# A fourth room for raw up weights in a Strassen-type gated network, the fourth rounded block kept inside the normed input, and the down weights' loads moved to GpSimd's queue

## The chip, the cores and the metric

The kernel runs on one core of one Trainium2 chip. The time is device microseconds of one execution: the median of three runs is 1200.07 us (1199.22 to 1203.46). The engines are named as in the profile: PE (matrix multiplication), PEld (its weight loads), DVE (vector engine), ACT (activation engine), POOL (GpSimd) and SP (the engine that here only issues DMAs). Each of them works through its own queue in order. A DMA is issued by one of these queues; a load that has to wait for its destination to come free waits at the head of its queue, and what is queued behind it waits too.

## The reference

Two residual layers on 512 tokens of width 1024, a state-space mixer in the first and forgetting attention in the second, each followed by a gated network. The gated network is what the change touches:

```python
def conv_ffn(h, w_up, conv_w, conv_b, w_down):
    up = h @ w_up                      # 1024 -> 2 x 2816
    a, b = jnp.split(up, 2, axis=-1)
    ...
    a_conv = conv_b
    for i in range(CONV_W):            # causal, width 3
        a_conv = a_conv + ap[:, i:i + S] * conv_w[i]
    return (jax.nn.silu(a_conv) * b) @ w_down
```

Its input h is the normed and modulated residual stream; the output is scaled by a gate and added to the stream. All of it is float32.

## The kernel before, in words

**Precision.** A float32 product is made of three faster ones. Each operand is cut into a rounded part ("hi", made by ACT, line 303) and the rest ("lo", source minus hi, made by DVE, line 304; together `put_parts`), and hi·hi, hi·lo and lo·hi are added up in PSUM. So every weight that reaches PE has passed through ACT and DVE first.

**The gated network** (`ffn`, lines 621 to 698, called once per layer: `l` is 0 and 1, called the first and the second network here). The hidden width 2816 is 22 tiles of 128; tile `f` has two weight matrices of 1024 x 128, number `2f` of the convolved branch and `2f+1` of the other, 512 KB each. The normed input `x` is a pair of tiles `a_hi`, `a_lo` of 128 partitions x 8 x 512 (8 blocks of 128 channels, 512 tokens). The tiles `f` = 0 to 3 go through a plain product (`product`, PE line 320). From `f` = 4 on `quarters` (line 548) takes the two matrices together.

**`quarters`** sees the two matrices as a 2 x 2 block matrix (a11, a12 the halves of matrix `2f` along the channels, a21, a22 those of `2f+1`) and `x` as 2 x 2 (b11, b12, b21, b22: halves of the channels by halves of the tokens), and forms the result with seven block products in place of eight. Of `x` itself it multiplies b11, b21 and b22 only; b12 (channel blocks 0 to 3, tokens 256 to 511) goes in through sums that `forms_x` made once. Each product is 12 matmuls of 256 columns (PE line 588). For one `f` the helpers do this: DVE makes four sums of 512 columns (line 556, tiles `sums`), ACT and DVE cut four weight blocks into hi and lo (a11 with a12, then two pairs of sums, 1024 columns each, then a22 alone, 512 columns), ACT copies three products (line 595, `nm_h`), DVE adds four results (line 556, `nm_t`), and the gate's elementwise work follows (lines 638 to 657). The a22 block is cut into a room of its own in the network's pool, one for hi and one for lo, which the next `f` uses again. `behind(*copied)` puts the cuts of one `f` after the last copy of the `f` before on ACT.

**The down product.** The 22 tiles are worked in groups (4, 4, 5, 4, 5 in the first network, 6, 5, 6, 5 in the second). While the tiles of one group go through the up products, the down products of the group before are spread between them, about two output blocks for each `f` (line 694). Only the last group's are made at the end.

**Rooms and queues.** `raw` (line 191) loads a weight matrix. Up weights go to the ring `raw` with three rooms (`RAW`), loaded by SP's queue (line 197). A room comes free when its last reader is done: for matrix `2f` that is the fourth sum on DVE (a12 minus the second sum), for matrix `2f+1` the cut of a22 on DVE. In the first network the down weights have a ring of their own, `rawd` with two rooms, loaded by SP's queue as well (line 194); their readers are ACT line 303 and DVE line 304. In the second network they go through the ring of three with the up weights.

**Work beside it.** During the first network DVE also reduces the modulation weights of later layers (`ada_units`, line 244): 1024 columns in one instruction (line 273), from one room `ada_raw`. Its next load is issued on POOL's queue (line 259) as soon as DVE is done with the room. `tick` calls place two of these per `f`.

**Order of the work.** The library that the kernel is written in fixes the order of every engine's queue when the program is built, from its own estimate of durations, and places semaphore waits for every read after a write, write after a read and reuse of a room. `issue_after` adds wishes to that order.

The change and the prediction's steps touch `raw`, `quarters`, and through them the loads at lines 194 and 197, the cuts at 303 and 304, and the sums at 556.

Of the kernel before, what the change touches and what calls it, by code (L numbers as in the profile page):

```python
# [9 lines left out]
F32 = mybir.dt.float32  # L10
F32R = mybir.dt.float32r
# [7 lines left out]
P = 128  # L19
D = 1024  # L20
KT = D // P
# [46 lines left out]
ROOM, ASIDE, VALUES = 9 * P, 22, 16  # L68
# [7 lines left out]
def part_of(pool, shape, name, tag, bufs, aside=0):  # L76

    _, n, w = shape
    t = pool.tile([P, ROOM if bufs == WB else n * w + P], F32R, name=name, tag=tag, bufs=bufs)
    return t[:, aside:aside + n * w].rearrange("p (n w) -> p n w", w=w)  # L80


class Trunk:
# [107 lines left out]
    def raw(self, shape, src, n=0):  # L191
        if self.room:
            t = self.bgpool.tile(shape, F32, name=self.room, bufs=2)
            self.nc.sync.dma_start(t, src)
            return t
        t = self.wpool.tile(shape, F32, name="raw", tag=("raw", "w_hi", "w_lo")[n], bufs=(RAW, WB, WB)[n])
        self.loads.dma_start(t, src)
        return t
# [349 lines left out]
    def quarters(self, pool, l, f, x, finish):  # L548

        nc = self.nc  # L550
        H, N = KT // 2, S // 2
        t1, t2 = HALVES
        a, b = (self.raw([P, KT, P], self.io["w_up"][l][2 * f + j]) for j in range(2))
        a11, a12, a21, a22 = a[:, :H], a[:, H:], b[:, :H], b[:, H:]
        c, d = (pool.tile([P, 2, H, P], F32, name="sums", bufs=2) for _ in range(2))
        sub = lambda o, u, v, op=ALU.subtract: nc.vector.tensor_tensor(o, u, v, op)  # L556
        w = {}
        copied = self.copied

        def parts(src, names, *where):  # L560
            hi, lo = (
                pool.tile([P, H * P + (P if n == "w_hi" else 32)], F32R, name=n, tag="e" + n)[:, ASIDE:ASIDE + H * P].rearrange("p (n w) -> p n w", w=P)
                if where else part_of(self.wpool, [P, len(names) * H, P], n, n, WB, ASIDE)
                for n in ("w_hi", "w_lo")
            )
            with self.behind(*copied):
                self.put_parts(hi, lo, src)
            for j, n in enumerate(names):
                w[n] = hi[:, j * H:(j + 1) * H], lo[:, j * H:(j + 1) * H]

        parts(a, ("a11", "a12"))
        sub(c[:, 0], a21, a22, ALU.add)
        sub(c[:, 1], c[:, 0], a11)
        parts(c.rearrange("p n k m -> p (n k) m"), ("s1", "s2"))
        sub(d[:, 1], a11, a21)
        sub(d[:, 0], a12, c[:, 1])
        parts(d.rearrange("p n k m -> p (n k) m"), ("s4", "s3"))
        parts(a22, ("a22",), pool)
        quarter = lambda k, t: tuple(v[:, k * H:(k + 1) * H, t] for v in x)
        xs = {"b11": quarter(0, t1), "b21": quarter(1, t1), "b22": quarter(1, t2)}  # L580
        for n, v in self.tx.items():
            xs[f"t{n}"] = v

        def times(o, wn, xn, first=True):
            (whi, wlo), (xhi, xlo) = w[wn], xs[xn]
            for k in range(H):
                for n, (wt, xt) in enumerate(((whi, xhi), (whi, xlo), (wlo, xhi))):
                    self.last_mm = nc.tensor.matmul(  # L588
                        o, wt[:, k], xt[:, k], start=(first and k == 0 and n == 0), stop=(k == H - 1 and n == 2),
                        skip_group_check=True,  # L590
                    )

        def copy(o, last=False):
            t = self.tmp.tile([P, N], F32, name="nm_h", bufs=4)
            a = nc.scalar.activation(t, o, AF.Copy)  # L595
            if last:
                self.copied = [a.ins]
            return t

        p1, p5 = (self.mm.tile([P, S], F32, name="mmp")[:, :N] for _ in range(2))  # L600
        p2, p4 = (self.aux.tile([P, S], F32, name="aux")[:, :N] for _ in range(2))
        oa, ob = (self.tmp.tile([P, S], F32, name="nm_t") for _ in range(2))
        times(p1, "a11", "b11")
        c1 = copy(p1)
        times(p5, "s1", "t1")
        c5 = copy(p5)
        times(p2, "a12", "b21")
        sub(oa[:, t1], p2, c1, ALU.add)
        times(p1, "s2", "t2", False)
        c2 = copy(p1, True)  # L610
        times(p5, "s4", "b22", False)
        sub(oa[:, t2], p5, c2, ALU.add)
        finish(2 * f, oa, slice(0, S))
        times(p4, "a22", "t4")
        c4 = copy(p4)
        times(p1, "s3", "t3", False)
        sub(ob[:, t2], p1, c5, ALU.add)
        sub(ob[:, t1], p1, c4)
        finish(2 * f + 1, ob, slice(0, S))
# [98 lines left out]
class Ew:  # L718
# [29 lines left out]
    def sub(self, a, b, out=None):  # L748
        return self.tt(a, b, ALU.subtract, out)
# [70 lines left out]
class S5(Trunk):  # L820
# [345 lines left out]
    def s5(self, i, nxt):  # L1166
# [7 lines left out]
        with ExitStack() as stack:  # L1174
# [120 lines left out]

            yhi = ylo = None
            raw, hi, lo, gps = {}, {}, {}, {}

            def part_hi(m):
# [597 lines left out]
```

## Time and profile before

| what | value |
|---|---|
| median of the runs (lowest to highest) | 1200.07 us (1199.22 to 1203.46) |
| the profiled execution's own time | 1197.47 us |
| its span, first to last instruction | 1195.7 us |
| PE busy | 1174.6 us (98%), 7983 matmuls |
| DVE busy | 1011.1 us (85%), 1836 instructions |
| ACT busy | 619.9 us (52%), 1186 instructions |
| POOL busy | 124.1 us (10%), 230 instructions |
| moved by DMA | 182.02 MB, mean 152 GB/s |

How to read it: times of views are microseconds from the start of the span. Matmuls overlap, so their durations add up to more than the span; a PE that is busy is not proof that it runs at its peak, but an idle PE is lost time. In the view of waits each row says which instruction waited for which, how long in total, how often, and the longest. In the view by windows each row is one stretch of time with the busy time of each engine in it (in brackets the number of instructions), the share of its clock that PE was granted, the share of the DMA engines and the rate. In the timeline a row is start, duration, engine, line, operation, output and inputs, and in square brackets the idle time before it and what ended it.

### The profile page before, as it was taken

To read this page: it belongs to the slowest core of one execution; us is meant where nothing else is said; L and a number is where in the kernel's file an instruction comes from. 1 tells how busy PE (TensorE), PEld (TensorE's weight loads), DVE (VectorE), ACT (ScalarE), POOL (GpSimd) and SP (SyncE) were. 2 spreads that over 40 slices of the span, in tenths; PEclk is the share of its full clock that TensorE was granted. 3 is DMA by queue.
4 is the path that set the end of the run, shared out by engine and by line. 5 is a ranking of instruction groups with operands and counts; after the bars stand their busy time and mean duration, and the time that the engine had idled before them with its cause. 6 is when DMAs were issued, how large, how long until landed. Compare 5 with 4: busy or idle time off the path is not lost.

```text
span 1195.7 us, 20776 instructions
## 1 busy us (share of the span) xinstructions
PE 1174.6 (98%) x7983; PEld 1021.7 (85%) x7983; DVE 1011.1 (85%) x1836; ACT 619.9 (52%) x1186; POOL 124.1 (10%) x230
## 2 busy tenths in 40 slices
PE   9999999999999899999999999999999999999997
PEld 4566678898999889999998788878989999999987
DVE  8989887889999989998786678867899887888865
ACT  3564644436554445455452566564456555545543
POOL 3231012100000000000000444330000000000000
PEclk9999999999999999999999999999999999999999
DMA  9588777721554445332454444433122342323331
GB/s 371 202 330 275 214 249 274 271 73 53 177 176 133 168 167 185 133 102 87 151 175 165 139 150 157 139 111 106 56 88 80 124 136 76 110 90 110 111 101 72
DMA packets 72115, 182.02 MB, mean 152 GB/s; under 512 B 23135, under 2 KB 25023, under 8 KB 70991
## 3 DMA queue, kind: packets, MB, share of 16 engines
q1 hardware_dynamic: 58767, 136.77, 34.5%
q0 software_dynamic: 11920, 43.26, 10.1%
q8 instruction: 63, 1.03, 0.3%
q10 hardware_dynamic: 1328, 0.66, 0.2%
q14 instruction: 37, 0.30, 0.1%
HBM read 173.73 MB, written 6.92 MB: 151 GB/s over the span
## 4 chain that ended last, share of the span: by engine, by line
PE 58%; issue 19%; DVE 12%; DMA 7%; ACT 1%; POOL 1%; SPq 0%; DVEq 0%; POOLq 0%; ACTq 0%
PE mmp L320 24%; PE mmp L588 12%; PE aux L588 5%; PE mmp L1277 4%; DVE w_lo L304 3%; DMA raw<-in_w_up 3%; PE mmp L1617 2%; PE aux L1035 1%; PE aux L1756 1%; PE mmp L229 1%; DVE sums L556 1%; PE aux L1776 1%; PE aux L1147 1%; DVE h L402 1%; DVE conv L640 1%
## 5 line engine op out<-in xcount | busy, mean ns | idle before, releaser
L304 DVE TENSOR_TENSOR w_lo<-raw,w_hi 128x1024 fp32r<-128x1024 f32 (+4 forms) x173 | 181.0, 1050 | 29.8 <-ACT w_hi L303 29.4
L303 ACT ACTIVATE w_hi<-raw 128x1024 fp32r<-128x1024 f32 (+4 forms) x173 | 154.0, 898 | 97.3 <-PE mmp L320 40.2
L320 PE MATMUL mmp<-ghi,w_hi 128*128 128x512 f32 (+1 forms) x412 | 147.5, 358 | 0.0
L320 PE MATMUL mmp<-glo,w_hi 128*128 128x512 f32 (+1 forms) x412 | 147.3, 358 | 0.0
L320 PE MATMUL mmp<-ghi,w_lo 128*128 128x512 f32 (+1 forms) x412 | 146.8, 356 | 0.0
L588 PE MATMUL mmp<-w_hi,w_lo 128*128 128x256 f32 x432 | 120.1, 278 | 3.3 <-DVE w_lo L304 3.3
L588 PE MATMUL mmp<-w_hi 128*128 128x256 f32 x432 | 120.1, 278 | 1.0 <-ACT nm_h L595 1.0
L588 PE MATMUL mmp<-w_lo,w_hi 128*128 128x256 f32 x432 | 119.7, 277 | 0.0
L320 PE MATMUL mmp<-a_hi,w_hi 128*128 128x512 f32 (+1 forms) x304 | 109.7, 364 | 0.0
L320 PE MATMUL mmp<-a_hi,w_lo 128*128 128x512 f32 (+1 forms) x304 | 107.9, 355 | 0.0
L320 PE MATMUL mmp<-a_lo,w_hi 128*128 128x512 f32 (+1 forms) x304 | 107.8, 356 | 0.0
L303 ACT ACTIVATE w_hi<-sums 128x1024 fp32r<-128x1024 f32 x80 | 83.9, 1058 | 44.3 <-DVE sums L556 38.9
L304 DVE TENSOR_TENSOR w_lo<-sums,w_hi 128x1024 fp32r<-128x1024 f32 x80 | 97.6, 1219 | 0.6 <-ACT w_hi L303 0.6
L595 ACT ACTIVATE nm_h<-mmp 128x256 f32<-128x256 f32 x108 | 40.3, 379 | 100.8 <-PE mmp L588 100.5
L320 PEld LDWEIGHTS mmp<-ghi,w_lo 128*128 128x128 f32 x412 | 77.4, 188 | 11.7
L320 PEld LDWEIGHTS mmp<-ghi,w_hi 128*128 128x128 f32 x412 | 77.3, 188 | 10.6
L320 PEld LDWEIGHTS mmp<-glo,w_hi 128*128 128x128 f32 x412 | 77.4, 188 | 10.2
L588 PEld LDWEIGHTS mmp<-w_hi,w_lo 128*128 128x128 f32 x432 | 81.5, 189 | 3.7 <-DVE w_lo L304 3.7
L588 PEld LDWEIGHTS mmp<-w_hi 128*128 128x128 f32 x432 | 81.7, 189 | 1.5 <-ACT nm_h L595 1.4
L588 PEld LDWEIGHTS mmp<-w_lo,w_hi 128*128 128x128 f32 x432 | 81.6, 189 | 0.0
L588 PE MATMUL mmp<-a_hi,w_lo 128*128 128x256 f32 x288 | 80.1, 278 | 0.8 <-DVE w_lo L304 0.8
L588 PE MATMUL mmp<-a_hi,w_hi 128*128 128x256 f32 x288 | 80.2, 278 | 0.6 <-ACT w_hi L303 0.6
(337 smaller groups left out, 3138.7 us busy)
## 6 DMA issues: line engine op xcount, KB each, us to landing
raw<-in_w_up SPq DMA_DIRECT2D x88, 512.0 KB, 3.7
ada_raw<-in_ada_t POOLq DMA_DIRECT2D x40, 512.0 KB, 4.1
raw<-in_ada_w POOLq DMA_DIRECT2D x24, 512.0 KB, 7.2
nf<-nfd SPq DMA_DIRECT2D x8, 1152.0 KB, 7.8
raw<-in_ada_w SPq DMA_DIRECT2D x16, 512.0 KB, 10.0
raw<-in_fox_qk SPq DMA_DIRECT2D x16, 512.0 KB, 3.6
raw<-in_w_down SPq DMA_DIRECT2D x24, 320.0 KB, 2.9
rawd<-in_w_down SPq DMA_DIRECT2D x24, 256.0 KB, 3.9
```

The costliest lines, as they stand in the source:

```text
L229: self.last_mm = nc.tensor.matmul(ps[32 * qq:32 * qq + 32, :], self.sc32[:, k, :], w[:, q * S:(q + 1) * S], start=(step is steps[0]), stop ...
L303: self.rounded = nc.scalar.activation(hi, src, AF.Copy).ins
L304: return nc.vector.tensor_tensor(lo, src, hi.bitcast(F32), ALU.subtract)
L320: self.last_mm = self.nc.tensor.matmul(o if len(xt.shape) == 2 else by_place(o), wt, xt, start=(k == 0 and n == 0), stop=(k == nk - 1 and ...
L402: add = self.nc.vector.scalar_tensor_tensor(h, ps, self.par[i][:, 16 + m:17 + m], h, op0=ALU.mult, op1=ALU.add,)
L556: sub = lambda o, u, v, op=ALU.subtract: nc.vector.tensor_tensor(o, u, v, op)
L588: self.last_mm = nc.tensor.matmul(o, wt[:, k], xt[:, k], start=(first and k == 0 and n == 0), stop=(k == H - 1 and n == 2), skip_group_che ...
L595: a = nc.scalar.activation(t, o, AF.Copy)
L640: c = nc.vector.scalar_tensor_tensor(t[:, d:], ps[:, :S - d], cw[:, 2 - d, f:f + 1], t[:, d:], op0=ALU.mult, op1=ALU.add)
L1035: nc.tensor.matmul(ps[:, :, cols], x[:, q, r].rearrange("p c j -> p (c j)"), both[:, :, planes, q, :], start=(r == 0), stop=(r == 1), skip ...
L1277: one = lambda k: nc.tensor.matmul(ps, w[m][:, k, :], x[:, k], start=(k == 0), stop=(k == KT - 1))
L1617: self.last_mm = nc.tensor.matmul(ps[q, b][:, :n], xt[:, k, tb], wt, start=(k == 0 and i == 0), stop=(k == KT - 1 and i == 2),)
```

## The change

Three edits.

1. In `quarters` the second matrix `2f+1` of odd `f` no longer goes through the ring of three rooms. It has a room of its own, `rawx`, in the network's pool, and SP's queue loads it as before. Even `f` are as they were.
2. The rounded a22 block and its rest no longer have rooms of their own in the pool. They are written into the b12 quarter of the normed input, `a_hi` and `a_lo`: for each of channel blocks 0 to 3, 128 columns from token 278 on. Nothing else is stored there once `forms_x` and the plain products have read it.
3. The down weights of the first network (`rawd`) are loaded by POOL's queue in place of SP's.

```diff
     def raw(self, shape, src, n=0):
         if self.room:
             t = self.bgpool.tile(shape, F32, name=self.room, bufs=2)
-            self.nc.sync.dma_start(t, src)
+            self.nc.gpsimd.dma_start(t, src)
             return t
...
-        a, b = (self.raw([P, KT, P], self.io["w_up"][l][2 * f + j]) for j in range(2))
+        a = self.raw([P, KT, P], self.io["w_up"][l][2 * f])
+        if f % 2:
+            b = pool.tile([P, KT, P], F32, name="rawx", bufs=1)
+            nc.sync.dma_start(b, self.io["w_up"][l][2 * f + 1])
+        else:
+            b = self.raw([P, KT, P], self.io["w_up"][l][2 * f + 1])
...
-        def parts(src, names, *where):
+        def parts(src, names, where=None):
             hi, lo = (
-                pool.tile([P, H * P + (P if n == "w_hi" else 32)], F32R, name=n, tag="e" + n)[:, ASIDE:ASIDE + H * P].rearrange("p (n w) -> p n w", w=P)
+                where[i][:, :H, N + ASIDE:N + ASIDE + P]
                 if where else part_of(self.wpool, [P, len(names) * H, P], n, n, WB, ASIDE)
-                for n in ("w_hi", "w_lo")
+                for i, n in enumerate(("w_hi", "w_lo"))
             )
...
-        parts(a22, ("a22",), pool)
+        parts(a22, ("a22",), x)
```

## The prediction

> **What bounds the kernel now.** The page first: is there idle time on PE at all, and do loads stand in the chain that ended last?
>
> ```profile
> span 1195.7 us, 20776 instructions
> PE 1174.6 (98%) x7983; PEld 1021.7 (85%) x7983; DVE 1011.1 (85%) x1836; ACT 619.9 (52%) x1186; POOL 124.1 (10%) x230
> PE mmp L320 24%; PE mmp L588 12%; PE aux L588 5%; PE mmp L1277 4%; DVE w_lo L304 3%; DMA raw<-in_w_up 3%; PE mmp L1617 2%; PE aux L1035 1%; PE aux L1756 1%; PE mmp L229 1%; DVE sums L556 1%; PE aux L1776 1%; PE aux L1147 1%; DVE h L402 1%; DVE conv L640 1%
> ```
>
> PE is idle for 1195.7 - 1174.6 = 21.1 us in all, so any edit that only removes waits is worth less than 2%. But loads of up weights (`raw<-in_w_up`) do stand in the chain. Where the idle time lies is told by the view by windows, for stretches of the first network (296 to 566 us) and one of the second (1030 to 1090):
>
> ```profile
> 296.00:368.50 72.50, 72.50 (x531) 68.14 (x530) 71.38 (x113) 40.45 (x66) 3.72 (x7) 1.00 0.49 164
> 368.50:468.00 99.50, 93.95 (x650) 86.96 (x649) 93.44 (x150) 47.60 (x78) 6.91 (x13) 0.98 0.46 160
> 468.00:500.70 32.70, 32.70 (x230) 30.31 (x229) 32.58 (x52) 17.59 (x28) 1.59 (x3) 1.00 0.54 182
> 1030.00:1090.00 60.00, 59.03 (x426) 54.98 (x425) 51.49 (x79) 32.46 (x52) 0.00 (x0) 1.00 0.34 107
> 435.90:439.30 3.40, 3.40 (x19) 3.40 (x18) 2.47 (x6) 1.55 (x3) 0.53 (x1) 0.50 0.30 100
> ```
>
> Columns: length, then busy time of PE, PEld, DVE, ACT, POOL, then PE's clock. In the second row PE loses 99.50 - 93.95 = 5.55 us, and the last row adds 3.40 us at half the clock, worth 1.70 us: 7.25 us together. DVE, with 93.44 us of work there, is idle for only 6.06 us: the stretch can't become shorter than 93.44 us unless DVE's work spills past its end. Before and after it (rows one and three) PE loses nothing although DVE is full: DVE is level with PE throughout. In the second network PE loses 0.97 us.
>
> Which waits are these? First PE's in the first network, then DVE's there and (first row of its own list) in the second:
>
> ```profile
> PE mmp L588 <- DVE w_lo L304: 4.1, 4, 2.0
> PE aux L588 <- DVE w_lo L304: 0.9, 1, 0.9
> PE mmp L588 <- ACT w_hi L303: 0.6, 1, 0.6
> DVE sums L556 <- DMA raw<-in_w_up: 3.6, 2, 2.0
> DVE sums L556 <- DMA raw<-in_w_up: 25.9, 13, 3.6
> ```
>
> PE waits for cut weights (4.1 + 0.9 + 0.6 = 5.6 us, the same loss), and DVE, which cuts them, waits for raw up weights. How a load gets late shows in the timeline:
>
> ```profile
> 388.06 0.69 DVE L556 TENSOR_TENSOR sums<-raw,sums 128x512 f32<-128x512 f32 x1
> 388.81 0.93 SPq L197 DMA_DIRECT2D raw<-in_w_up  x2
> 393.28 0.69 DVE L556 TENSOR_TENSOR sums<-raw 128x512 f32<-128x512 f32 x1 [1.58 <-DMA raw<-in_w_up]
> 424.98 1.29 DVE L556 TENSOR_TENSOR sums<-raw 128x512 f32<-128x512 f32 x2 [1.99 <-DMA raw<-in_w_up]
> ```
>
> The fourth sum ends at 388.75 and frees the first matrix's room; at 388.81 SP issues the load that waited for it, which is the next f's second matrix (three rooms: two of this f, the next f's first). DVE needs it for the next f's first sum and gets it at 393.28, having stood for 1.58 us. 1.58 + 1.99 is the 3.6 us.
>
> **Part by part.**
>
> *The fourth room.* With four rooms in turn (three and `rawx` for odd f), each matrix of the first network has its room one f earlier, against the 4.5 us from issue (388.81) to use (393.28). The 3.6 us of DVE waits go. What is DVE's other idle time in that stretch? By forms:
>
> ```profile
> L273 DVE CUSTOM_DVE_ANT_0 ada_raw<-ada_raw,c_row 128x1024 f32<-128x1024 f32 x13 | 15.9, 1220 | 0.9 <-DMA ada_raw<-in_ada_t 0.9
> L304 DVE TENSOR_TENSOR w_lo<-sums,w_hi 128x1024 fp32r<-128x1024 f32 x12 | 14.6, 1220 | 0.2 <-ACT w_hi L303 0.2
> L556 DVE TENSOR_TENSOR sums<-raw 128x512 f32<-128x512 f32 x12 | 8.0, 686 | 3.6 <-DMA raw<-in_w_up 3.6
> L556 DVE TENSOR_TENSOR nm_t<-aux,nm_h 128x256 f32<-128x256 f32 x6 | 2.5, 421 | 1.1 <-PE aux L588 0.9
> ```
>
> The third row counts two sums for each f, so the stretch holds 6 f's, 99.5 / 6 = 16.6 us each: that is how much earlier a load can start. The 0.2 and 1.1 us are waits for ACT and PE that were late themselves; I let 1.2 of these 1.3 go as well. Sum for the first network: 3.6 + 1.2 = 4.8 us. Ends: 0 (other waits take the place) and 6.06 (DVE never idle); I take 4.8 since DVE is the limit there and this much of its idle time has a named cause. PE's 7.25 us are not reached, because DVE is next.
>
> In the second network the ring also carries down weights (no `rawd`), so a pair of f's puts seven or so loads through three rooms, and one of these leaves the ring. DVE waits long there (25.9 us) but has slack, 51.49 of 60.00 us, and PE lost 0.97 us. I book 0.7; ends 0 and 0.97.
>
> *The clock.* The 3.40 us at half clock start where a long PE wait ends:
>
> ```profile
> 435.52 0.38 PE L588 MATMUL mmp<-w_hi,w_lo 128*128 128x256 f32 x1 [1.99 <-DVE w_lo L304]
> ```
>
> I take the drop as a consequence of this 1.99 us wait. [...]
>
> *The a22 block within x.* The same two instructions (ACT, DVE) on the same 512 columns, written as four pieces of 128 columns; PE loads 128 columns at a time from either place.
>
> ```profile
> L304 DVE TENSOR_TENSOR w_lo<-raw,w_hi 128x512 fp32r<-128x512 f32 x6 | 4.1, 687 | 0.0
> L303 ACT ACTIVATE w_hi<-raw 128x512 fp32r<-128x512 f32 x6 | 3.8, 631 | 5.4 <-PE aux L588 3.9 <-DVE w_lo L304 1.3 <-DMA raw<-in_w_up 0.3
> 297.83 0.69 DVE L304 TENSOR_TENSOR w_lo<-raw,w_hi 128x512 fp32r<-128x512 f32 x1
> 296.35 0.28 PE L588 MATMUL mmp<-a_hi,w_hi 128*128 128x256 f32 x1
> ```
>
> I book 0. It can't gain, having the same elements, and the wait for the a22 product of the f before (3.9 us on ACT) stays, as there is still one room. Upper end: no row shows a write in four pieces; if it cost what 1024 columns cost (1220 in place of 687 ns), 6 x 0.53 = 3.2 us on DVE in the busy stretch. Nearest is the same operation on 512 columns, hence 0. The first f of a network must now wait for the last plain product's reads; its block was cut at 297.83, after that product had given way to line 588 at 296.35, so this costs nothing.
>
> *POOL's queue for `rawd`.* The transfers stay; only the issuing queue changes, and on POOL they are queued with `ada_raw`, whose waiting load holds up what is behind it.
>
> ```profile
> raw<-in_w_up SPq DMA_DIRECT2D x88, 512.0 KB, 3.7
> ada_raw<-in_ada_t POOLq DMA_DIRECT2D x40, 512.0 KB, 4.1
> rawd<-in_w_down SPq DMA_DIRECT2D x24, 256.0 KB, 3.9
> 407.23 0.93 SPq L194 DMA_DIRECT2D rawd<-in_w_down  x2
> 412.45 0.53 POOL L259 DMA_DIRECT2D ada_raw<-in_ada_t  x1 [7.10 <-DVE ada_s L273]
> 420.17 1.14 ACT L303 ACTIVATE w_hi<-rawd 128x512 fp32r<-128x512 f32 x2
> SPq L194 <- DVE w_lo L304: 56.1, 28, 8.7
> POOL ada_raw L259 <- DVE ada_s L273: 160.6, 22, 13.8
> ```
>
> From issue (407.23) to the reader on ACT (420.17) there are 12.94 us; less 0.53 for POOL's issue and 4.1 to land, 8.3 us of margin, with POOL nearly idle. SP loses waits of 56.1 us, during which it could not issue up weights. Both sides are hidden as long as the margin holds: 0. Ends: 0 and the price of the rival below.
>
> *Sum:* -4.8 - 0.7 + 0 + 0 = -5.5 us. Against the profiled execution's own time, 1197.47 us, that is 1191.97; the median of the runs shown stands 2.6 us higher, and the same difference gives 1200.07 - 5.5 = 1194.6 us.
>
> **The rivals.** About 0.5% (6 us) is what a measurement of this kernel can tell from no change.
>
> *DVE takes over with its other load.* `ada_raw` has one room, and its two reductions of an f lie about 5 us apart: reload issued after the reduction (0.53 us), 4.1 us to land. If DVE runs denser, six of the 13 reductions in the stretch may wait 0.4 us each, 2.4 us given back: 1200.07 - 5.5 + 2.4 = 1197.0. For it: 0.9 us of such waits exist. Against: only 0.9 us over all 13.
>
> *Everything freed.* PE limits again, because DVE's work spills into the later stretch: 5.55 + 1.70 + 0.97 = 8.2 us, 1191.9. [...] Against: 32.58 of 32.70 us leave DVE no room up to 500.7.
>
> *Slower, by POOL's order.* If a `rawd` load is queued behind the `ada_raw` load that waits longest, it comes late once that wait exceeds the 8.3 us of margin. The mean wait is 160.6 / 22 = 7.3 us, the longest 13.8, so up to 5.5 us late, 2.75 in the middle, on ACT, which then also copies products late. If half of the 11 f's (two reductions each) are hit: 5.5 x 2.75 = 15 us, net of the gain 1200.07 - 5.5 + 15 = 1209.6. Against: both waits are for DVE's own order, and a `rawd` room comes free between two reductions.
>
> *Slower, by one room.* The change would not do what it says if the waits treated the whole of x as one room. Then an f's first product, which reads x, stands behind the cut of its a22:
>
> ```profile
> 383.67 0.28 PE L588 MATMUL mmp<-a_hi,w_hi 128*128 128x256 f32 x1
> 388.67 0.68 DVE L304 TENSOR_TENSOR w_lo<-raw,w_hi 128x512 fp32r<-128x512 f32 x1
> 251.59 0.36 PE L320 MATMUL mmp<-a_hi,w_hi 128*128 128x256 f32 x1
> 255.72 0.97 ACT L470 ACTIVATE a_hi<-nm_h,par 128x256 fp32r<-128x256 f32 x2 [1.79 <-DVE nm_h L467]
> ```
>
> 389.35 - 383.67 = 5.7 us for each of 36 f's, 204 us: about 1404. Against: PE reads `a_hi` from 251.59 on while ACT still writes other parts of it at 255.72, so parts are kept apart.
>
> **How the numbers follow.** Forecast 0.55 (a gain of 4 to 7.3 us, half of it beyond 6), everything freed 0.15, DVE takes over 0.19, POOL's order 0.08, one room 0.03. Faster: 0.275 + 0.15, rounded to 0.43; same: 0.275 + 0.19, rounded to 0.46; slower: 0.11. The two slower cases are the 0.11 left out of the range. Its lower end is everything freed (1191.9) less 2.4 for the spread between the profiled time and the median, 1189.5; its upper end is no gain at all plus the lesser half of the a22 bound (1.6), 1201.6.
>
> **What would show it.** Right: no rows of `sums` waiting for `raw<-in_w_up` in the first network, the stretch around 368 to 468 with DVE idle below 2 us, no half-clock window, and `rawd` on POOL without ACT waiting for it. Wrong: `ada_raw` waits above 2 us on DVE (it takes over), ACT's cut of `rawd` waiting for its load (POOL's order), a22's cut on DVE above 0.75 us (four pieces cost), or line 588's first product of an f waiting for `w_lo` (one room).

## The result and the profile after

| | before | after |
|---|---|---|
| median of 5 runs each on one chip (lowest to highest) | 1200.07 us (1198.33 to 1203.46) | 1190.88 us (1190.09 to 1195.64) |
| ratio after / before, 95% interval | | 0.9925 [0.9897, 0.9953] |
| the profiled execution's own time | 1197.47 us | 1190.3 us |

The change made the kernel faster by 0.75%, 9.2 us by the medians and 7.2 us by the two profiled executions; the forecast was 5.5. Two executions are left out of every median and ratio of this document, because they ran far longer than the others of their kernel: one of e5, at a granted clock of 0.55 (1962.69 us), and one of e2 (4183.32 us). The page of the kernel after:

```profile
span 1188.5 us, 20777 instructions
PE 1172.6 (99%) x7983; PEld 1020.1 (86%) x7983; DVE 1011.6 (85%) x1836; ACT 619.7 (52%) x1186; POOL 141.7 (12%) x262
...
rawx<-in_w_up SPq DMA_DIRECT2D x18, 512.0 KB, 4.1
```

The engines have the same work to do as before. POOL alone has more, 262 instructions for 230: the issues of `rawd`. Where the time came from is told by windows. Columns: length, busy time of PE, PEld, DVE, ACT, POOL, PE's clock, DMA share, GB/s. First the kernel before, with one row each for the first network, the attention stage and the second network (a network's row runs from the first product that reads the normed input to the next norm):

```profile
251.50:589.10 337.60, 332.05 (x2330) 308.62 (x2330) 313.22 (x497) 175.68 (x282) 12.22 (x23) 0.99 0.41 137
589.10:845.30 256.20, 252.50 (x1610) 219.29 (x1608) 193.43 (x469) 137.24 (x304) 63.18 (x83) 1.00 0.42 141
845.30:1176.00 330.70, 329.73 (x2331) 306.71 (x2332) 278.21 (x428) 176.95 (x283) 0.00 (x0) 1.00 0.31 96
```

Then the kernel after: the stretch of the first network on which the prediction rested, and the same three rows.

```profile
368.50:468.00 99.50, 98.26 (x711) 91.86 (x710) 99.36 (x161) 51.30 (x84) 14.52 (x27) 1.00 0.53 178
251.40:582.90 331.50, 330.07 (x2330) 306.91 (x2329) 311.73 (x497) 175.82 (x282) 28.48 (x53) 1.00 0.43 137
582.90:840.80 257.90, 254.15 (x1608) 220.19 (x1608) 195.41 (x469) 137.23 (x304) 64.29 (x83) 1.00 0.43 142
840.80:1169.00 328.20, 328.20 (x2332) 306.07 (x2332) 278.12 (x428) 176.30 (x284) 0.00 (x0) 1.00 0.31 95
```

The first network is 337.60 - 331.50 = 6.1 us shorter, the second 330.70 - 328.20 = 2.5 us, and the attention stage, which the change doesn't touch, 257.90 - 256.20 = 1.7 us longer. In the stretch 368.5 to 468, DVE now works 99.36 of 99.50 us (before 93.44): it is full, and PE still loses 99.50 - 98.26 = 1.24 us there.

The views of waits of the kernel after: PE in the first network (290 to 566 us), DVE there, then DVE in the second (855 to 1185 us):

```profile
PE mmp L593 <- DVE w_lo L304: 1.2, 2, 0.6
...
DVE w_lo L304 <- ACT w_hi L303: 7.6, 9, 2.2
DVE nm_t L561 <- PE aux L593: 2.9, 3, 2.2
DVE conv L645 <- ACT conv L643: 0.9, 1, 0.9
DVE ada_raw L273 <- DMA ada_raw<-in_ada_t: 0.5, 1, 0.5
...
DVE sums L561 <- DMA raw<-in_w_up: 7.5, 5, 4.1
```

PE's waits for cut weights fell from 5.6 to 1.2 us. In the first network the row `sums <- raw<-in_w_up` is gone, and in the second it fell from 25.9 to 7.5 us. The timeline of the kernel after shows how early a load of the fourth room now is:

```profile
372.41 0.69 DVE L304 TENSOR_TENSOR a_lo<-rawx,a_hi 128x512 fp32r<-128x512 f32 x1
...
373.17 0.33 SPq L556 DMA_DIRECT2D rawx<-in_w_up  x1
...
388.10 0.70 DVE L561 TENSOR_TENSOR sums<-rawx 128x512 f32<-128x512 f32 x1
```

The cut of a22 ends at 373.10 and frees the room, SP issues the reload at 373.17, and DVE reads it at 388.10. From issue to use there are 14.9 us, where the kernel before had 4.5.

### The profile page after: what moved, and what is told of

It reads as the page before. It is cut to its first block, busy times and chain, and to the rows that moved or that the text cites. A ratio compares the mean times of both kernels' runs of the same rounds, so it can differ in the third digit from the quotient of the medians.

```text
span 1188.5 us, 20777 instructions
## 1 busy us (share of the span) xinstructions
PE 1172.6 (99%) x7983; PEld 1020.1 (86%) x7983; DVE 1011.6 (85%) x1836; ACT 619.7 (52%) x1186; POOL 141.7 (12%) x262
## 4 chain that ended last, share of the span: by engine, by line
PE 83%; DVE 10%; DMA 3%; issue 2%; ACT 1%; SPq 0%; DVEq 0%; ACTq 0%
PE mmp L320 39%; PE mmp L593 17%; PE aux L593 7%; PE mmp L1282 4%; DVE w_lo L304 3%; PE mmp L1622 2%; PE mmp L1324 2%; PE aux L1761 2%; PE aux L1040 1%; PE mmp L229 1%; PE aux L1152 1%; DVE ada_raw L273 1%; DVE sums L561 1%; PE aux L1781 1%; PE aux L1141 1%
## 5 line engine op out<-in xcount | busy, mean ns | idle before, releaser
L304 DVE TENSOR_TENSOR w_lo<-raw,w_hi 128x1024 fp32r<-128x1024 f32 (+3 forms) x137 | 159.4, 1169 | 42.2 <-ACT w_hi L303 41.6
L303 ACT ACTIVATE w_hi<-raw 128x1024 fp32r<-128x1024 f32 (+3 forms) x137 | 132.1, 969 | 85.5 <-PE mmp L320 46.3
L402 DVE SCALAR_TENSOR_TENSOR h<-mmp,par,h 128x512 f32<-128x512 f32 (+1 forms) x104 | 69.1, 667 | 14.3 <-PE mmp L320 13.9
```

What stands on the lines that cost most here:

```text
L303: self.rounded = nc.scalar.activation(hi, src, AF.Copy).ins
L304: return nc.vector.tensor_tensor(lo, src, hi.bitcast(F32), ALU.subtract)
L402: add = self.nc.vector.scalar_tensor_tensor(h, ps, self.par[i][:, 16 + m:17 + m], h, op0=ALU.mult, op1=ALU.add,)
```

## The experiments

Each kernel below was compared with runs of the kernel before on the same chip, whose medians are 1199.45 us (for e1 to e4), 1199.01 (e5 to e8) and 1200.35 (e9 to e12). Of every profiled execution I took the length of four stages from the trace, each from the first sum of squares of one norm (line 419) to that of the next:

| kernel | median, us | ratio [95%] | first network | attention | second network |
|---|---|---|---|---|---|
| before | 1200.07 | | 345.2 | 248.5 | 338.1 |
| after | 1190.88 | 0.9925 [0.9897, 0.9953] | 339.1 | 250.3 | 335.6 |
| after, again (e4) | 1190.42 | 0.9928 [0.9915, 0.9940] | 338.6 | 251.0 | 335.6 |
| rooms, `rawd` on SP (e1) | 1192.44 | 0.9947 [0.9928, 0.9965] | 339.1 | 251.0 | 335.6 |
| POOL's queue alone (e2) | 1199.51 | 1.0004 [0.9991, 1.0016] | 344.4 | 250.3 | 337.3 |
| no fourth room (e3) | 1198.89 | 0.9998 [0.9978, 1.0017] | 345.1 | 251.0 | 339.6 |
| fourth room, first network only (time of e5, stages of e12) | 1192.54 | 0.9947 [0.9927, 0.9966] | 339.0 | 251.8 | 337.4 |
| fourth room, second network only (e6) | 1195.77 | 0.9971 [0.9957, 0.9985] | 344.3 | 248.6 | 335.6 |
| before, reductions thinned (e7) | 1191.57 | 0.9937 [0.9917, 0.9957] | 335.9 | 250.9 | 338.0 |
| after, reductions thinned (e8) | 1186.50 | 0.9895 [0.9875, 0.9915] | 336.4 | 249.1 | 335.8 |
| the same, again (e10) | 1188.00 | 0.9899 [0.9881, 0.9917] | 335.9 | 249.7 | 335.7 |
| the same, `rawd` on SP (e9) | 1187.92 | 0.9903 [0.9885, 0.9921] | 336.2 | 249.7 | 335.7 |

The networks' lengths repeat within about 1 us wherever the same network is built the same way, with one exception: the second network without the room and with the a22 block in `x` took 339.6 us in e3 and 337.4 in e12. The attention stage, built alike in all of them, lies anywhere from 248.5 to 251.8.

**Theory and rivals.** Theory: the fourth room does it, in the first network because DVE, level with PE, no longer stands for a load, in the second because the ring is short of rooms. Rivals: POOL's queue does it (SP's waiting loads of down weights no longer hold up the up weights), or the a22 block does.

### One part undone or alone (e1 to e4)

e1, the kernel after with `rawd` back on SP's queue:

```diff
-            self.nc.gpsimd.dma_start(t, src)
+            self.nc.sync.dma_start(t, src)
```

> The changed kernel with one part undone: the first network's down weights stay on SP's queue; the fourth room and the a22 block within x are kept. Theory (the fourth room earns it): no row of sums waiting for raw<-in_w_up in the first network, and a gain over the kernel before of 6 to 9 us, within 1.5 us of the changed kernel. Rival (freeing SP's queue of the down loads' waits earns half or more): a gain of 2 to 4 us only, and up loads that are issued late behind the waits at line 194.

e2, the kernel before with only the queue changed (the same line the other way round):

> The kernel before with one part done alone: the first network's down weights are loaded by POOL's queue; three rooms and the a22 block in its own room as before. Theory (the fourth room earns it): within 1.5 us of the kernel before, with DVE still waiting 3 to 4 us for raw<-in_w_up in the first network, since the second matrix's load still waits for the fourth sum. Rival (SP's queue earns it): 3 to 6 us faster.

e3, the kernel after without the fourth room, so the a22 block in `x` and POOL's queue are left:

```diff
-        if f % 2:
+        if False:
```

> The changed kernel without the fourth room: a22 within x and the down loads on POOL stay, the second matrix of odd f goes through the ring of three again. Theory (the fourth room earns it): the kernel before's time within 1.5 us, PE waiting 4 to 6 us for cut weights in the first network. Rival (the two other parts, by another order of the instructions): 4 us or more faster than the kernel before.

e4, the kernel after, unchanged, on the chip of these three:

> The changed kernel once more, on the same chip as the three others, so that they can be set against it. 7 to 9 us faster than the kernel before by either theory; if it is under 5 us, the first measurement held 2 us or more of chance.

Measured: e2 and e3 are equal to the kernel before (1.0004 and 0.9998), e1 keeps most of the gain. So without the room neither POOL's queue alone nor that queue together with the a22 block is worth anything measurable. The waits say the same. DVE's and PE's rows of e3 in the first network:

```profile
DVE sums L561 <- DMA raw<-in_w_up: 3.7, 2, 2.2
...
PE mmp L593 <- DVE w_lo L304: 4.2, 4, 1.9
PE aux L593 <- DVE a_lo L304: 1.2, 1, 1.2
PE mmp L593 <- ACT w_hi L303: 0.5, 1, 0.5
```

These are the waits of the kernel before (3.6; 4.1, 0.9 and 0.6), now at the new place of the block. Between e1 and e4 lie 2.0 us, more than the 1.5 that the theory of e1 allowed, but their intervals overlap: whether POOL's queue adds to the room's gain is left to e9.

### The room in one network (e5, e12, e6)

```diff
-        if f % 2:
+        if f % 2 and l == 0:
```

> The changed kernel with the fourth room in the first network only; the second network's up weights go through the ring of three. Theory: the first network keeps its gain of about 6 us in its own stretch, the second network goes back to the 338 us of the kernel before, so 4 to 7 us faster than before and 2 to 3 us slower than the changed kernel. Rival (the second network's loads were hidden, as the prediction nearly had it, 0.7 us): within 1 us of the changed kernel.

> The fourth room in the first network alone, once more, for its profile. Theory (each network's part comes from its own fourth room): first network 338.5 to 339.5 us as in the kernel after, second network 337.5 to 338.5 as in the kernel before; VectorE waits for raw up weights some 26 us in the second network and not at all in the first. Rival (the second network's part comes from the a22 block or from POOL's queue): second network 335.6 us here too.

And with `l == 1`, the second network only:

> The changed kernel with the fourth room in the second network only. Theory: the second network keeps its 2.5 us, the first one goes back to about 345 us with PE waiting 4 to 6 us for cut weights: 1.5 to 3.5 us faster than the kernel before. Rival (hidden loads in the second network): within 1 us of the kernel before.

e12 is the kernel of e5 once more, and the stages are read from it. Its one execution took 1196.47 us, longer than the median of e5; 2.9 us of this lie ahead of the first network, which starts at 246.7 us there and at 243.8 in the kernel after. The effects are separate and add up within their intervals: -0.53% and -0.29% make -0.82%, against -0.75% of the change. By stages the room shortens its own network by 6.2 us (345.2 to 339.0) or 2.5 us (338.1 to 335.6) and leaves the other within 1 us of before. Because the second network without the room ranges from 337.3 (e2) to 339.6 us (e3), the room's part there is known no better than 1.7 to 4.0 us. e12's row of DVE in the second network, then e6's rows of DVE and PE in the first:

```profile
DVE sums L561 <- DMA raw<-in_w_up: 25.5, 13, 3.7
```

```profile
DVE sums L561 <- DMA raw<-in_w_up: 2.8, 2, 2.0
...
PE mmp L593 <- DVE w_lo L304: 2.6, 3, 1.8
PE aux L593 <- DVE a_lo L304: 2.0, 1, 2.0
```

Each network without the room keeps the waits it had. e6 has the a22 block in `x` and POOL's queue in the first network as well, so this is a second sign that those two carry nothing there.

### Is the late load a cause or a consequence? (e7, e8)

If DVE is the limit of the first network, giving it spare time should do what the room does. The reductions of modulation weights (1.22 us each) can be spread over more of the stage: of the two `tick` calls for each f, the one in `gated` is made for odd f only. e7 is that edit in the kernel before, e8 in the kernel after.

```diff
                     if plain and f >= groups[0]:
                         self.evac = [c.ins]
-                        self.tick(ticks)
+                        if f % 2:
+                            self.tick(ticks)
```

> The kernel before, with the reductions of the modulation weights thinned out: of the two that go with an f in the first network, the one at the convolved branch is placed at odd f only, so that the 24 spread over more f's. The work is the same. Theory (late loads cost there because DVE has no slack): DVE still waits for raw<-in_w_up, but PE's waits for cut weights fall from 5.6 us to under 2.5, and the time falls by 3 to 6 us. Rival (a late load costs by its own length, whatever DVE's load): PE waits 4 us or more, and the time is within 1.5 us of the kernel before.

> The changed kernel with the same thinning of the reductions. Theory (what is left of PE's waits in the first network is DVE being full): the last 1.2 us of waits for cut weights go, and the first network's stretch falls by 1 to 2.5 us below the changed kernel's; 8 to 11 us faster than the kernel before. Rival (what is left has another cause): within 0.7 us of the changed kernel.

e7's stretch 368.5 to 468, by windows:

```profile
368.50:468.00 99.50, 99.50 (x722) 93.26 (x721) 98.98 (x157) 53.31 (x88) 5.29 (x10) 1.00 0.48 159
```

With three rooms only, PE is never idle here, and the first network takes 335.9 us, 3.2 less than in the kernel after. DVE's list of waits in this network has no row for `raw<-in_w_up` any more; that it would still stand there was expected and was wrong. The time fell by 7.4 us, more than the 3 to 6 expected, and the first network by 9.3 us, more than by the room: the thinning also moves 6 of the 24 reductions (7.3 us of DVE's work) past 500.7 us, where DVE has slack (busy 56.11 of the 65.30 us to 566 in the kernel before). The late load of the kernel before was thus part of a circle: DVE runs late, so its fourth sum frees the room late, so the load is late, so DVE runs later. The fourth room cuts the circle at the load, the thinning at DVE. Both cure the same loss: with both (e8) the first network takes 336.4 us, no less than with the thinning alone (and 2.7 us less than in the kernel after, where up to 2.5 was expected). In the second network, which has no reductions, the thinning does nothing (338.0), and the room's 2.2 us (338.0 to 335.8) come on top. So e8 is the best version, 1186.5 us, 12.5 below before where 8 to 11 was expected.

### POOL's queue once more, and the repeat (e9, e10)

e10 is e8 again; e9 is e8 with `rawd` back on SP (the edit of e1).

> The kernel after with the thinned reductions, and the raw down weights of the first network issued by SP again. Theory (POOL's queue matters only where SP's waiting loads of down weights hold up a raw up weight that VectorE is about to read): with the thinned reductions PE had no waits for cut weights left in the first network (336.4 us), so the queue is worth nothing there; within 1 us of the thinned kernel with POOL's queue, 1186.5 us, thus 1186 to 1188, first network 335.5 to 337.5 us. Rival (POOL's queue is worth about 2 us by itself, as 1192.4 against 1190.4 suggested): 1188.5 or more, first network 338 us, and PE waits for cut weights again.

> The kernel after with the thinned reductions, once more, as the yardstick of the run before it on the same chip. Theory: 1186.5 us within 1 us, ratio to before 0.9885 to 0.991; the first network 336 to 337 us, the second 335.5 to 336. Rival (the first result was a lucky chip): above 1188.5 us.

1187.92 and 1188.00: with DVE no longer full, POOL's queue is worth nothing that can be measured. e10 came out 1.5 us above e8, just outside the theory's 1 us, with a ratio to before that agrees (0.9899 against 0.9895). Whether the queue is worth something between nothing and 2 us in the unthinned kernel stays open.

### The clock (e11)

The kernel after; in the second network the fourth sum of f = 8, 12 and 16 is repeated 8, 12 and 16 times more (36 instructions in all), so that PE has to wait.

```diff
-        sub(d[:, 0], a12, c[:, 1])
+        for _ in range(1 + ({8: 8, 12: 12, 16: 16}.get(f, 0) if l else 0)):
+            sub(d[:, 0], a12, c[:, 1])
```

> The kernel after; in the second network the fourth difference of f = 8, 12 and 16 is repeated 8, 12 and 16 times more (about 0.69 us each: 5.5, 8.2 and 11 us of VectorE's time), so that PE has to wait three times, longer each time; VectorE's slack there is some 2.6 us for each f. Nothing else differs, and the repeated difference writes the same values. Theory (an idle time of PE of about 2 us or more halves its clock for 3.4 us): each PE idle time of 2 us or more is followed by one stretch of 3.4 us at half clock, those below 1.9 us by none. [...] The time is that of the idle times and 1.7 us for each drop above 1190.4: 1196 to 1206 us.

The steps were not graded: in the second network PE waited for a cut weight twice, once for 1.1 us and once for 6.0.

```profile
PE mmp L594 <- ACT w_hi L303: 7.1, 2, 6.0
```

So e11 alone couldn't settle the length that matters. But the drop at the longer wait didn't fit the theory, as the windows show:

```profile
1063.00:1066.41 3.41, 0.00 (x0) 0.00 (x0) 3.31 (x6) 0.00 (x0) 0.00 (x0) 1.00 0.00 0
1066.42:1069.83 3.41, 1.84 (x7) 1.73 (x8) 2.98 (x4) 2.31 (x3) 0.00 (x0) 0.50 0.44 154
1069.84:1073.24 3.40, 3.40 (x18) 3.40 (x17) 3.40 (x6) 2.84 (x3) 0.00 (x0) 0.50 0.63 204
1073.25:1076.65 3.40, 3.40 (x18) 2.85 (x17) 3.40 (x7) 0.63 (x1) 0.00 (x0) 1.00 0.57 219
```

The clock is at 0.50 from 1066.42 on, while PE is still idle (for 1.57 us of that row), and stays there for two stretches of 3.41 us, not one. This is what such stretches show in the kernel before, e12, e6 (two pairs) and e3:

```profile
432.51:435.92 3.41, 1.43 (x13) 1.23 (x12) 3.37 (x6) 0.69 (x2) 0.00 (x0) 1.00 0.44 154
435.93:439.34 3.41, 3.41 (x18) 3.41 (x18) 2.48 (x6) 1.59 (x3) 0.53 (x1) 0.50 0.30 100
```

```profile
148.78:152.18 3.40, 1.59 (x43) 1.25 (x41) 3.37 (x4) 3.40 (x9) 1.05 (x2) 1.00 0.66 170
152.19:155.60 3.41, 3.41 (x41) 1.63 (x36) 3.31 (x5) 0.60 (x1) 0.00 (x0) 0.50 0.96 309
```

```profile
399.69:403.10 3.41, 1.65 (x14) 1.46 (x13) 3.41 (x5) 0.63 (x1) 0.41 (x1) 1.00 0.48 154
403.11:406.51 3.40, 3.40 (x31) 3.34 (x30) 3.40 (x7) 3.27 (x6) 0.53 (x1) 1.00 0.63 169
416.76:420.16 3.40, 1.41 (x12) 1.21 (x11) 3.40 (x7) 1.06 (x1) 0.54 (x1) 1.00 0.03 10
420.17:423.57 3.40, 3.40 (x18) 3.40 (x17) 3.40 (x6) 2.10 (x3) 0.00 (x0) 0.50 0.92 311
```

```profile
397.85:401.26 3.41, 2.23 (x20) 2.03 (x18) 3.41 (x7) 1.37 (x3) 0.53 (x1) 1.00 0.15 50
401.27:404.67 3.40, 2.72 (x23) 2.72 (x24) 3.40 (x6) 1.69 (x4) 0.13 (x1) 1.00 0.47 119
```

PE is idle for 3.41 - 1.43 = 1.98 us (before), 3.40 - 1.59 = 1.81 us (e12) and 3.40 - 1.41 = 1.99 us (e6, second pair) of the first row, and the second is at half clock. With 3.41 - 1.65 = 1.76 us (e6, first pair) it isn't. Nor does the clock fall in e3, whose longest wait, 1.9 us (1.18 and 0.68 us of the two rows), is longer than the 1.81 us of e12: e3's clock is 1.00 over the whole of 368.5 to 468.

At the end of the kernel less idle time stood ahead of a drop. This is the stretch of the kernel before ahead of the half clock at 1190.27:

```profile
1186.86:1190.26 3.40, 1.95 (x16) 1.52 (x14) 2.15 (x11) 1.27 (x4) 0.00 (x0) 1.00 0.22 83
```

PE is idle for 3.40 - 1.95 = 1.45 us of it; in the kernel after it is 3.41 - 1.92 = 1.49 us (1179.89 to 1183.30), with half clock from 1183.31. PE's work there is sums of one column (line 419) and transposes (line 501), not the products of the networks. So these runs show no length of idle time that draws the border, and why one wait brings a drop and another doesn't is not shown.

What a drop costs the kernel is not shown either. Half of 3.41 us is 1.7 us of PE's work, but the first network took 345.2 and 344.3 us with a drop in it (before and e6, clock 0.98 from 368.5 to 468) and 344.4 and 345.1 us without one there (e2 and e3, clock 1.00).

## Why the prediction was right, and where its sizes were not

**DVE is level with PE, and loads of up weights make it late: right.** No sum waits for `raw<-in_w_up` in the first network, and DVE's idle time in the stretch fell from 6.06 to 0.14 us. What I had not seen is that the load's lateness is itself DVE's lateness (e7).

**First network, booked 4.8, measured 6.1 us: the term was too small.** The step that failed is the sum 3.6 + 1.2. It left DVE 1.26 us of its idle time in the stretch, 0.9 of it waits for `ada_raw`, and these went too, as the row of the reductions in the kernel after shows (the stretch 368.5 to 468):

```profile
L273 DVE CUSTOM_DVE_ANT_0 ada_raw<-ada_raw,c_row 128x1024 f32<-128x1024 f32 x14 | 17.1, 1223 | 0.0
```

That the upper end, 6.06 us, lies so near to 6.1 is partly luck. Followed f by f (the end of DVE's `glo` in both traces), the kernel after is 7.2 us ahead at the sixteenth f and 6.1 at the network's end, where DVE waits longer than before. By the rows of the whole network, DVE's idle time fell from 337.60 - 313.22 = 24.38 to 331.50 - 311.73 = 19.77 us, by 4.6, and the other 1.5 us are DVE's busy time, with the same 497 instructions. Where that part comes from is not shown. "PE's 7.25 us are not reached, because DVE is next" held: 1.24 us of PE's idle time stay in the stretch, with DVE at 99.36 of 99.50 us. e8 and e10 show that DVE was the reason: there PE is idle for 0.01 and 0.00 us.

```profile
368.50:468.00 99.50, 99.50 (x732) 93.72 (x731) 97.47 (x154) 52.85 (x87) 12.40 (x23) 1.00 0.49 162
```

(e10; DVE has 2 us to spare in the same stretch.)

**Second network, booked 0.7 with an upper end of 0.97, measured 2.5: outside its ends.** The step that failed is "PE lost 0.97 us": that is PE's idle time. Of the 2.5 us, 0.97 were idle time that vanished; the other 1.53 are PE's busy time, 329.73 before and 328.20 after, with the same matmuls. The profile models the ends of matmuls (mean 0.28 us where the next starts 0.11 us later), so a gap shorter than what is modelled beyond the next start counts as busy. Taken from the starts of all matmuls of that stage, the time beyond the usual 0.113 us (256 columns) or 0.227 us (512 columns) fell by 2.2 us. The largest pieces of before, 0.62 and 0.68 us, stand ahead of the matmuls at 1063.35 and 1080.53 after products into `aux`. How a load reached PE there is in ACT's list of waits of the kernel before (855 to 1185 us), and in PE's:

```profile
ACT w_hi L303 <- DVE sums L556: 26.2, 25, 3.2
...
PE mmp L588 <- ACT nm_h L595: 1.0, 2, 0.5
```

DVE waited 25.9 us for loads, ACT 26.2 us for DVE's sums, and copied products to `nm_h` late, for which PE waited. "DVE has slack" was true and did not help, since ACT's order carried the wait on. That the small gaps are that chain too is argued, not shown; that the gain as a whole belongs to the room is shown by e12 (337.4 us without it) and e6 (335.6 with it), its size within the 1.7 to 4.0 us above.

**The clock:** in the kernel after no half-clock stretch is left before the one at its end, from 1183.31 on, so the drop went with the wait of 1.99 us, as read from the trace. The forecast held nothing for it, since DVE's 6.06 us of idle time bounded the first network's term. Not every long wait brought a drop: with longest waits of 1.7 us (e2) and 1.9 us (e3) in the first network, the clock from 368.5 to 468 was 1.00.

**The a22 block, booked 0: right.** e3, with POOL's queue as well, equals before, and the cut into four pieces (DVE by forms, kernel after, 368.5 to 468) costs 694 and 695 against 687 ns:

```profile
L304 DVE TENSOR_TENSOR a_lo<-rawx,a_hi 128x512 fp32r<-128x512 f32 x4 | 2.8, 694 | 0.0
...
L304 DVE TENSOR_TENSOR a_lo<-raw,a_hi 128x512 fp32r<-128x512 f32 x3 | 2.1, 695 | 0.0
```

Its part in the change is space: the block's rooms, 128 x (512 + 128) and 128 x (512 + 32) numbers of 4 bytes, are 4.6 KB of each partition, and `rawx` takes 4 KB. The room without that edit was not tried, so that it needs this space is not shown.

**POOL's queue, booked 0: right** alone (e2) and with DVE relieved (e9); beside the room in the kernel after, between 0 and 2 us stay open (e1 against e4). ACT waits for no `rawd` load in the kernel after.

**The rivals.** `ada_raw` did not take over: DVE's waits for it in the first network are 0.5 us. "POOL's order" and "one room" would have shown ACT waiting for `rawd` or PE's first product waiting for the cut; neither is there. "Everything freed", 1191.9 us, came nearest to the measured 1190.9 in size, though not by its mechanism: PE is still short of weights in the first network. The gain lies above the 4 to 7.3 us that the prediction gave its own case; the networks' part above the forecast came from the first network (1.3 us) and the second (1.8 us, 1.5 of it busy time). The lower end of the range took 2.4 us for the spread between profiled time and median, which the same text puts at 2.6; 1189.3 would have been consistent, and changes nothing here.

**Profile against median.** The networks gave 8.6 us, the medians 9.2, the profiled executions 7.2: the difference is mainly the attention stage, 1.7 us longer in that execution of the kernel after. Since this stage took 248.5 us in the profiled execution of before, and 250.3 and 250.9 in e2 and e7, whose attention stage is the kernel before's, it is scatter and no effect of the change.

## What to carry to other kernels

A late load need not mean too few rooms: see first whether its consumer frees the room late because it is full; then spreading that engine's optional work can do as much as another room or more (e7), and where both help, they may cure the same loss and not add up (e8). Let all of the limiting engine's idle time go if one cause feeds it; but take neither its idle time nor PE's as a hard ceiling, since in both networks a part of the gain (1.5 us of DVE's time in the first, 1.5 of PE's in the second) stood in the profile as busy time. Before crediting a change with a microsecond, compare the stages it does not touch.

## What was not expected of the hardware

- PE's granted clock fell to 0.50 after 1.98 us (before), 1.99 us (e6) and 1.81 us (e12) of idle time in the 3.41 us ahead, each time for 3.41 us, and for twice that at a wait of 6.0 us (e11). After 1.76 us (e6) and a wait of 1.9 us (e3) it didn't. At the kernel's end, with transposes and one-column sums, 1.45 us (before) and 1.49 us (after) stood ahead of a drop. What decides it is not shown.
- The attention stage, with the same work, took 248.5 to 251.8 us from execution to execution, and the medians of one kernel on two chips differed by 1.5 us (1186.5 and 1188.0).
- A load of 512 KB took 4.1 us in the median to land in the room of its own against 3.6 in the ring, on the same queue; why is not shown. It costs nothing where it is issued 14.9 us ahead of its use, as in the timeline above.
